# Sample-group attention of a one-step decoder: split float32r products over the whole array, or plain float32 products on 32-column quarters

## The chip, the cores and the metric

The kernel runs on one core of one Trainium2 chip. The metric is the device time of one execution in microseconds (us): the median of three runs before is 3056.04 us (3052.62 to 3064.1). Engines go by short names: PE (TensorE's matmuls), PEld (its weight loads), DVE (VectorE), ACT (ScalarE), POOL (GpSimd), SP (SyncE, which issues most DMAs). PSUM is the memory that PE writes.

## The reference, cut to what matters

One layer of a hybrid decoder runs for two groups of tokens with the same weights: a prompt of 512 tokens, and a sample group of 8 batches x 4 steps, 32 tokens. The change touches only work of the sample group:

```python
# stick-breaking attention, 8 heads x 128, 512 paged keys per batch and the 4 own ones
z = einsum('bqhd,bkhd->bhqk', q, k) * scale + b_h
survive = reverse_cumsum(log_stay) - log_stay
o = einsum('bhqk,bkhd->bqhd', exp(log_sigmoid(z) + survive), v)
# cross attention, 4 heads x 128, 256 memory keys per batch
attn = softmax(einsum('bshd,bmhd->bhsm', xq, mem_k) * 128 ** -0.5)
xo = einsum('bhsm,bmhd->bshd', attn, mem_v)
# gated delta rule: new state per batch and head
state = g_i * state + einsum('bhcd,bhce->bhde', k_i, v_new)
```

Everything is float32. Every batch has keys, values and states of its own, so each product with them has four query rows a head and no more.

## The kernel before, in words

**Dense work.** The projections hold 128 weight columns in the array and stream 544 tokens (prompt and sample) past them in two halves of 272. To have nearly float32's exactness from float32r operands, each operand is split into a high and a low part (`weights`, line 187; `split`, line 231), and three products are made: L208 (`products`) in the first half of the program, L1530 in the cross-attention's output projection, L1647 in the feed-forward part, where Winograd's scheme lowers the number of products.

**Side work.** All attention, of both groups, is written as Python generators that a class `Side` (line 391) hands out in small steps between the dense blocks. A step yields two estimates: PE time, and time until its results are there. `tick` is called after each dense block with that block's estimated PE time (0.68 us in `products`); it adds credit (that time times `ratio`) and runs steps while credit lasts, but a generator is picked again only when its estimated latency has gone by. So the yields set the order in which instructions are written, and a scheduler then fixes each engine's static order. `drain` runs what is left with nothing between.

**The sample group's attention.** `sb_sample` (line 575) does four heads, twice. It calls `sample_logits` (line 661) for two heads at a time, 16 units each of 256 keys, then `sample_values` (line 708) for 32 pages of 128 values. `cross_sample` (line 1424) calls the same two for the memory keys: twice 8 units, then 16 blocks of values. In all there are 80 units of logits, 64 pages of values and 16 blocks of memory values.

- A unit of logits: four PE transposes (L960) bring 256 keys of two heads to PSUM; `parts` (line 652) makes the high part (ACT cast, L656) and the low part (DVE subtraction, L657); four float32r matmuls of 256 columns (L699) multiply them. The stationary operand is a 128-column window of `win` that holds the high and the low part of the queries in the batch's eight columns and zeros elsewhere (POOL, L669 to L675), so all batches add up in one PSUM tile.
- A page of values: `parts` splits it the same way, then two float32r matmuls with 32 stationary columns and 512 streamed ones (L750). In `cross_sample` values are not split: one plain float32 matmul for a block.
- The two parts are summed by matmuls with 0/1 matrices: `selz` at L630 and L1460, `selv` at L757.

Pages go through a pool of seven tiles (`c.load`, tag `load`); SP issues their DMAs. In `sb_sample` a tile is free again when `parts` has read it.

**State update.** `gdn_sample` (line 1136) ends with 16 matmuls (L1246) for eight heads and two halves of the batches, each with 32 rows of the array (`tile_position=(hh * 32, 0)`), one in a step.

**Where it runs.** The two `sb_sample` generators are handed out from about 690 us on, between the last projections of `sb_project` and the gate projections; their last products stand at 1080 us. `cross_sample` runs between L1530's products of the first half of the tokens, and `side.drain()` finishes it before the second half begins (in `cross`, line 1482).

Of the kernel before, what the change touches and what calls it, by code (L numbers as in the profile page):

```python
# [15 lines left out]
P = 128  # L16
# [54 lines left out]
def build_consts(c):  # L71
# [45 lines left out]
    # rows (head of two, 7 - batch, part, step) to columns (head of two, batch, step), both parts summed  # L117
    c.selw = ones("selz", [P, 192], 0.0)
    c.selz = c.selw[:, 64:128]
    for part in range(2):  # L120
        sel(c.selz, [[-64, 2], [8, 8], [-1, 4]], 1, -56 - 4 * part, ALU.not_equal, 1.0)
    # rows (batch of four, part, head, step) to columns (head, batch of four, step): the head's own, both parts summed
    c.selv = ones("selv", [P, 64], 0.0)
    for part in range(2):
        sel(c.selv, [[-4, 4], [-32, 4], [-1, 4]], 1, -16 * part, ALU.not_equal, 1.0)
# [14 lines left out]
def head_rows(c):  # L140
    """Per-head scalars: columns (chunk, head) on every partition, and two columns with rows (head, batch, step)."""
# [45 lines left out]
def weights(c, w, k0, nk, c0, n=P, kept=False, eng=None):  # L187
    """A block of weights, split exactly into two parts of 12 bits each: a pair for every feature block."""
# [13 lines left out]
def products(c, ps, w, k, act, first, last, n=P):  # L202
    """One block of a projection: w^T act, exact but for the product of the two low parts."""
# [11 lines left out]
def project(c, w, k0, c0, acts, n=P, step=8):  # L215
    """PSUM [n, 2, 272] = (rows k0.. of w, columns c0..c0+n)^T acts"""
# [14 lines left out]
def split(c, x, g, hi=None, lo=None):  # L231
    """x * g (g per partition) as two exact parts."""
# [13 lines left out]
class Stats:  # L246
    """Sum of squares over all features, for every token, on every partition."""
# [15 lines left out]
    def rstd(self, name, scale=None):  # L263
        """(mean + EPS) ** -0.5; with scale, what was added is scaled by it, and so is the root's reciprocal."""
# [81 lines left out]
def x_rstd(c, ss):  # L346
    """The reciprocal roots of the tokens' mean squares, from columns to rows on every partition."""
# [21 lines left out]
def first_projections(c):  # L369
    """Loads the tokens and projects them on the first head's q and k, feature block by feature block."""  # L370
# [20 lines left out]
class Side:  # L391
    """Work of the mixers, handed out in small steps between the blocks of the projections.

    A step yields (tensor engine time, time until its results are there), both estimates in us."""
# [6 lines left out]
    def put(self, g, low=False, tiles=None):  # L401
        """tiles: where the work takes its temporary tiles (float32, float32r) from, if not from the usual ones"""
# [51 lines left out]
    def finish(self, e, steps=1e9):  # L454
        """Runs one work to its end, or until so many of its steps are done."""
# [5 lines left out]
    def drain(self, some=None):  # L461
        """Runs all that is left, or until some is done."""
# [70 lines left out]
    # the sums of the keys behind, a block of keys after the other, each token's in its own column  # L533
# [21 lines left out]
def stick(c, z, n, sp=None):  # L555
    """softplus(z) and log(sigmoid(z)), each over n columns"""
# [18 lines left out]
def sb_sample(c, g):  # L575
    """Stick-breaking attention of the sample group, four heads: 512 paged keys and its own."""
# [12 lines left out]
    # own keys: rows (head, batch, step)  # L589
# [28 lines left out]
    # paged keys: columns (page, head, batch, step)  # L618
    psz = c.aux()
    for h2 in range(2):  # L620
# [6 lines left out]
        nc.scalar.copy(zt[:, :512], ps)  # L627
        for p in range(PAGES):
            o = p * P + h2 * 64
            nc.tensor.matmul(psz[:, o : o + 64], zt[:, p * P : (p + 1) * P], c.selz, start=True, stop=True)  # L630
        yield 0.9
# [20 lines left out]
def parts(c, src, vector=True):  # L652
    """src [P, 512] as two exact parts."""
# [7 lines left out]
def sample_logits(c, q, h0, load, n, ps=None, col=0):  # L661
    """Products of two heads' queries (q: columns (head, batch, step)) with n blocks of 256 keys of every batch.

    Returns PSUM with rows (head, 7 - batch, part of q, step); load(b, i): [keys, (2 blocks, 2 heads, d)]."""
    nc = c.nc
    nb, win = 2, []
    for b0 in range(0, NB, nb):
        w = c.tp("win")
        nc.gpsimd.memset(w[:, : nb * 192].bitcast(F32), 0.0)  # L669
        for b in range(b0, b0 + nb):  # L670
            o = (b - b0) * 192 + (NB - 1 - b) * 8
            d = w[:, o : o + 256].rearrange("p (h x) -> p h x", h=2)
            x = q[:, h0 * 32 : (h0 + 2) * 32].rearrange("p (h b t) -> p h b t", h=2, b=NB)[:, :, b]
            nc.gpsimd.tensor_copy(d[:, :, 0:4], x)
            nc.gpsimd.tensor_sub(d[:, :, 4:8], x, d[:, :, 0:4].bitcast(F32))  # L675
            win += [[w[:, (b - b0) * 192 + hh * 64 :][:, :P] for hh in range(2)]]
        yield 0.0, 0.3
    first = ps is None
    if first:
        ps = c.aux()  # L680
# [3 lines left out]
    def ahead():  # L684
        if units:
            nxt.append(parts(c, transposes(c, load(*units.pop(0)))))
# [5 lines left out]
    for u in range(NB * n):  # L692
        b, i = divmod(u, n)
        k2 = nxt.pop(0)
        ahead()
        for hh in range(2):
            for j, k in enumerate(k2):
                o = col + i * 256
                nc.tensor.matmul(  # L699
                    ps[:, o : o + 256], win[b][hh], k.rearrange("p (g h k) -> p h g k", g=2, h=2)[:, hh],  # L700
                    start=first and u == 0 and hh == 0 and j == 0,
                    stop=b == NB - 1 and hh == 1 and j == 1, skip_group_check=True,
                )
        yield 0.9, 0.4
# [3 lines left out]
def sample_values(c, w, n, load, split=True):  # L708
    """Sums of n blocks of 128 values of every batch with the weights w (columns (block, head, batch, step)).

    With split, both are taken in two exact parts.

    Returns PSUM [d, (head, batch, step)]; load(b, i): [keys, (4 heads, d)]."""
    nc = c.nc
    win = []
    for i in range(0, n, 2):
        t = (c.tp if split else c.tt)("win")
        for j in range(2):
            x = w[:, (i + j) * P : (i + j + 1) * P].rearrange("p (h b t) -> p b h t", h=4, b=NB)
            d = t[:, j * 256 : (j + 1) * 256].rearrange("p (b u h t) -> p b u h t", b=NB, u=2, h=4)  # L720
            nc.scalar.copy(d[:, :, 0], x)
            if split:
                nc.vector.tensor_sub(d[:, :, 1], x, d[:, :, 0].bitcast(F32))
            else:
                nc.gpsimd.memset(d[:, :, 1], 0.0)
        win.append(t)
    yield 0.1
    pso = c.aux()
    units = [(b, i) for b in range(NB) for i in range(n)]
    nxt = []  # L730

    def ahead():
        if units:
            v = load(*units.pop(0))
            nxt.append(parts(c, v) if split else [v])

    ahead()
    ahead()
    ahead()
    yield 0.0  # L740
    for half in range(2):
        o = c.tt("os")
        for b4 in range(4):
            b = half * 4 + b4
            ps = c.aux()
            for i in range(n):
                vs = nxt.pop(0)
                for j, v in enumerate(vs):
                    x = (i % 2) * 256 + b * 32
                    nc.tensor.matmul(ps[:32], win[i // 2][:, x : x + 32], v, start=i == 0 and j == 0, stop=i == n - 1 and j == len(vs) - 1)  # L750
                ahead()
                yield 0.45, 0.4
            nc.scalar.copy(o[b4 * 32 : b4 * 32 + 32, :512], ps[:32])
        yield 0.0, 0.8
        for h in range(4):
            x = h * 32 + half * 16
            nc.tensor.matmul(pso[:, x : x + 16], o[:, h * P : (h + 1) * P], c.selv[:, h * 16 : h * 16 + 16], start=True, stop=True)  # L757
# [4 lines left out]
def load_pages(c, cache, pages, h0, nh):  # L762
    """[keys, (page, head, d)] of the given pages (indices into the table)."""
# [11 lines left out]
def gates(c, acts, rstd):  # L775
    """Decay and beta of the gated delta rule, with tokens on partitions."""
# [4 lines left out]
    # prompt: columns (a|b, chunk, head); sample: columns (a|b, stack), rows (head, batch, step)  # L781
# [28 lines left out]
    # running sums of log decay, totals, and their exponentials  # L810
# [22 lines left out]
    # per (head, batch) of the sample stacks, on every partition  # L833
# [7 lines left out]
def silu(c, x, out):  # L841
    """out = x * sigmoid(x), with exp and ln alone"""
# [1104 lines left out]
```

## Time and profile before

| | |
|---|---|
| median of 3 runs | 3056.04 us (3052.62 to 3064.1) |
| span of the profiled execution | 3059.9 us (its time beside that is not listed) |
| PE, PEld busy | 95%, 91% of the span |
| DVE, ACT, POOL busy | 70%, 45%, 55% |
| instructions on PE | 22118 matmul records |
| DMA | 392.67 MB, 128 GB/s over the span |
| mean granted TensorE clock | 0.983 |

A plain float32 matmul is one instruction of the program and two records in the profile (two passes, each with its own weight load); a float32r matmul or a transpose is one record. A record's duration includes the time until its results are written, which overlaps the next one; what a matmul costs a busy PE is the distance from its start to the next start. The timeline merges neighbours of one kind: a row gives the start of the first, the time to the end of the last, and their number.

### The profile page before, as it was taken

The numbers are of one execution on the slowest core, as the hardware profiler recorded it, in microseconds if no ns is written. First come the engines' busy times: TensorE is split into PE (matmuls) and PEld (weight loads), VectorE is DVE, ScalarE is ACT, GpSimd is POOL, SyncE is SP. The second block draws the span as 40 slices with busy tenths as digits, with TensorE's granted clock in tenths as the row PEclk, the third lists the DMA queues.
The fourth block names the chain that finished last, engine by engine and source line by source line (L and its number), as shares of the span: only waits on it lengthen the run. The fifth ranks groups of instructions, "written<-read, shape, count | busy, mean of one in ns | idle before, by whom it ended". The sixth has DMA issues, their size and how long they took to land.

```text
span 3059.9 us, 58347 instructions
## 1 busy us (share of the span) xinstructions
PE 2900.2 (95%) x22118; PEld 2789.1 (91%) x22118; DVE 2134.3 (70%) x3339; ACT 1363.5 (45%) x2600; POOL 1671.8 (55%) x1784
## 2 busy tenths in 40 slices
PE   8999999999999999999799999999999989988898
PEld 7999998889899999999689999999999989988797
DVE  6776775655655655366687777777777888888865
ACT  5544453435645654245543343333333344334333
POOL 3211122312112100032378988898888977999997
PEclk9999999999999999999899999999999999999999
DMA  7323233544535765423434344333434354344343
GB/s 212 95 80 85 75 88 99 144 137 147 173 105 151 227 197 150 127 81 116 161 117 127 118 122 123 121 117 118 125 118 123 116 179 132 110 131 127 119 137 105
DMA packets 619505, 392.67 MB, mean 128 GB/s; under 512 B 36475, under 2 KB 572360, under 8 KB 619224
## 3 DMA queue, kind: packets, MB, share of 16 engines
q1 hardware_dynamic: 596904, 355.95, 39.6%
q10 hardware_dynamic: 22320, 32.99, 3.0%
q8 instruction: 174, 2.85, 0.4%
q14 instruction: 107, 0.88, 0.1%
HBM read 334.17 MB, written 54.68 MB: 127 GB/s over the span
## 4 chain that ended last, share of the span: by engine, by line
POOL 27%; PE 20%; DVE 8%; issue 4%; DMA 4%; ACT 2%; SPq 0%; POOLq 0%; ACTq 0%; DVEq 0%
PE mm L208 7%; POOL u L1615 6%; POOL u L1613 6%; POOL u L1614 5%; PE mm L1647 5%; POOL u L1616 5%; PE aux L1647 4%; DVE wl L1621 3%; DMA u<-in_w_gate_up 2%; DVE pr L1591 2%; PE aux L1342 2%; POOL acc L1670 1%; PE mm L1530 1%; POOL x L1572 1%; PE aux L960 1%
## 5 line engine op out<-in xcount | busy, mean ns | idle before, releaser
L1621 DVE TENSOR_TENSOR wl<-u,wh 128x768 fp32r<-128x768 f32 (+1 forms) x528 | 752.5, 1442 | 315.9 <-ACT wh L1620 213.6
L1647 PE MATMUL mm<-pr,wh 128*128 128x272 f32 x4224 | 830.6, 292 | 41.6 <-DVE acc L1663 25.3
L1620 ACT CAST wh<-u 128x768 fp32r<-128x768 f32 (+1 forms) x528 | 488.8, 943 | 826.5 <-PE aux L1647 295.4
L1647 PEld LDWEIGHTS mm<-pr,wh 128*128 128x128 f32 x4224 | 669.4, 191 | 50.5 <-DVE acc L1663 20.3
L1647 PE MATMUL aux<-pr,wh 128*128 128x272 f32 x3168 | 626.9, 292 | 17.7 <-DVE acc L1669 6.7
L1647 PE MATMUL mm<-pr,wl 128*128 128x272 f32 x2112 | 615.7, 292 | 22.5 <-DVE wl L1621 22.5
L208 PE MATMUL mm<-ah,wh 128*128 128x272 f32 (+1 forms) x2464 | 538.6, 298 | 5.7 <-ACT ah L321 4.6
L1647 PEld LDWEIGHTS aux<-pr,wh 128*128 128x128 f32 x3168 | 506.8, 192 | 21.7 <-DVE acc L1669 8.6
L208 PE MATMUL mm<-al,wh 128*128 128x272 f32 (+1 forms) x2464 | 524.3, 291 | 0.7 <-DVE al L239 0.7
L208 PE MATMUL mm<-ah,wl 128*128 128x272 f32 (+1 forms) x2464 | 515.6, 290 | 0.1
L1647 PE MATMUL aux<-pr,wl 128*128 128x272 f32 x1584 | 460.9, 291 | 2.0 <-DVE wl L1621 2.0
L1647 PEld LDWEIGHTS mm<-pr,wl 128*128 128x128 f32 x2112 | 403.3, 191 | 28.4 <-DVE wl L1621 28.4
L208 PEld LDWEIGHTS mm<-ah,wh 128*128 128x128 f32 (+1 forms) x2464 | 391.9, 189 | 28.8 <-issue 8.5
L197 DVE TENSOR_TENSOR wl<-wr,wh 128x512 fp32r<-128x512 f32 (+1 forms) x366 | 264.0, 725 | 195.9 <-ACT wh L196 186.7
L208 PEld LDWEIGHTS mm<-al,wh 128*128 128x128 f32 (+1 forms) x2464 | 389.6, 188 | 5.4 <-issue 2.0
L208 PEld LDWEIGHTS mm<-ah,wl 128*128 128x128 f32 (+1 forms) x2464 | 386.2, 188 | 2.5 <-DVE wl L197 0.5
L196 ACT CAST wh<-wr 128x512 fp32r<-128x512 f32 (+1 forms) x366 | 224.3, 615 | 336.6 <-PE mm L208 272.6
L1613 POOL TENSOR_TENSOR u<-u 128x256 f32<-128x256 f32 x264 | 277.3, 1050 | 140.8 <-DMA u<-in_w_gate_up 90.2
L1615 POOL TENSOR_TENSOR u<-u 128x256 f32<-128x256 f32 x264 | 323.2, 1224 | 0.0
L1616 POOL TENSOR_TENSOR u<-u 128x256 f32<-128x256 f32 x264 | 308.5, 1169 | 19.1
L1647 PEld LDWEIGHTS aux<-pr,wl 128*128 128x128 f32 x1584 | 303.7, 192 | 2.6 <-DVE wl L1621 2.4
L1614 POOL TENSOR_TENSOR u<-u 128x256 f32<-128x256 f32 x264 | 270.4, 1024 | 0.0
(518 smaller groups left out, 3809.1 us busy)
## 6 DMA issues: line engine op xcount, KB each, us to landing
u<-in_w_gate_up SPq DMA_DIRECT2D x352, 256.0 KB
wr<-in_w_in SPq DMA_DIRECT2D x108, 512.0 KB
u<-in_w_down SPq DMA_DIRECT2D x176, 256.0 KB
v<-hT SPq DMA_DIRECT2D x66, 272.0 KB
page<-in_cache_sb_k SPq DMA_DIRECT2D x128, 128.0 KB
page<-in_cache_sb_v SPq DMA_DIRECT2D x64, 256.0 KB
wr<-in_w_out SPq DMA_DIRECT2D x32, 512.0 KB
hT<-x ACTq DMA_DIRECT2D x44, 272.0 KB
```

Of the source, the lines that this page charges most:

```text
L196: nc.scalar.copy(hi[:, :m, :n], raw[:, k : k + m, :n])
L197: nc.vector.tensor_sub(lo[:, :m, :n], raw[:, k : k + m, :n], hi[:, :m, :n].bitcast(F32))
L208: c.nc.tensor.matmul(ps[:n, h, :HT], l[:, :n], r[:, h * HT : (h + 1) * HT], start=first and i == 0, stop=last and i == 2,)
L1342: nc.tensor.matmul(ps[:, :256], l, r, start=k == 0 and n == 0, stop=k == 7 and n == 2)
L1591: nc.vector.tensor_sub(lo[:, o : o + n * HT], x[:, : n * HT], hi[:, : n * HT].bitcast(F32))
L1613: nc.gpsimd.tensor_add(s1, a21, a22)
L1614: nc.gpsimd.tensor_sub(s3, a11, a21)
L1615: nc.gpsimd.tensor_sub(s2, s1, a11)
L1616: nc.gpsimd.tensor_sub(s4, a12, s2)
L1620: nc.scalar.copy(hi, u[:, o : o + n])
L1621: nc.vector.tensor_sub(lo, u[:, o : o + n], hi.bitcast(F32))
L1647: nc.tensor.matmul(ps, l[:, cols], r, start=u + i == 0 and j == 0, stop=u + i == n - 1 and j == 2)
```

## The change

- **Logits.** Keys are no longer split: ACT copies the transposed keys (`kT`). For a unit, four plain float32 matmuls of 128 columns are issued, one for each quarter of 32 array columns (`tile_position=(0, x * 32)`): quarter x takes head x % 2 and block x // 2 of the keys. A quarter's stationary operand has 32 columns, the batch's four queries and 28 zeros. The window is made once for all batches, and the step after it yields (0.0, 3.0) where four steps yielded (0.0, 0.3).
- **Summing.** At L630's place two transposes take the place of four matmuls for each pair of heads. In `cross_sample` four matmuls with 64 array columns each take the place of two.
- **Values.** Pages are no longer split: a step takes four pages (two batches x two pages) in four plain float32 matmuls on the four quarters, straight from the DMA's tile. Five pages are asked for ahead, where three were. One ACT copy of 128 rows takes the place of four of 32 rows, and `selv`'s matmuls double in number (8 columns each, where it was 16).
- **State update.** Two heads' matmuls, on two different groups of 32 rows, stand next to each other.
- The file's comments are gone, so the change's line numbers are a little lower: L203 is L208 of before, L949 is L960, L1527 is L1530.

```diff
 def sample_logits(c, q, h0, load, n, ps=None, col=0):
...
+    w = c.tt("win")
+    nc.gpsimd.memset(w[:, :512], 0.0)
+    win = w[:, :512].rearrange("p (b h x) -> p b h x", b=NB, h=2)
+    for b in range(NB):
+        x = q[:, h0 * 32 : (h0 + 2) * 32].rearrange("p (h b t) -> p h b t", h=2, b=NB)[:, :, b]
+        nc.gpsimd.tensor_copy(win[:, b, :, b * 4 : b * 4 + 4], x)
+    yield 0.0, 3.0
...
-            nxt.append(parts(c, transposes(c, load(*units.pop(0)))))
+            pt = transposes(c, load(*units.pop(0)))
+            k = c.tt("kT")
+            nc.scalar.copy(k[:, :512], pt)
+            nxt.append(k)
...
-        k2 = nxt.pop(0)
+        k = nxt.pop(0)
+        o = col + i * P
+        for x in range(4):
+            nc.tensor.matmul(
+                ps[x * 32 : x * 32 + 32, o : o + P], win[:, b, x % 2, :], k[:, x * P : (x + 1) * P],
+                start=u == 0 and col == 0, stop=b == NB - 1, skip_group_check=True, tile_position=(0, x * 32),
+            )
         ahead()
-        for hh in range(2):
-            for j, k in enumerate(k2):
...
-        yield 0.9, 0.4
+        yield 0.7, 0.4
...
-def sample_values(c, w, n, load, split=True):
+def sample_values(c, w, n, load):
...
+    todo = [(b2 * 2 + b, i + j) for b2 in range(4) for i in range(0, n, 2) for b in range(2) for j in range(2)]
...
+    for _ in range(5):
+        ahead()
     yield 0.0
-    for half in range(2):
+    for b2 in range(4):
+        ps = c.aux()
+        for i in range(0, n, 2):
+            for g in range(4):
+                b, j = divmod(g, 2)
+                nc.tensor.matmul(
+                    ps[g * 32 : g * 32 + 32], win[i // 2][:, j, b2 * 2 + b], nxt[g], start=i == 0, stop=i == n - 2,
+                    skip_group_check=True, tile_position=(0, g * 32),
+                )
+            del nxt[:4]
+            for _ in range(4):
+                ahead()
+            yield 1.2, 0.6
         o = c.tt("os")
...
+        nc.scalar.copy(o[:, :512], ps)
         yield 0.0, 0.8
```

And in `gdn_sample`:

```diff
-    for hh in range(4):
...
+    for h2 in range(2):
         for w in range(2):
...
+            for hh, _, ps in two:
+                rows = slice(hh * 32, (hh + 1) * 32)
+                nc.tensor.matmul(
+                    ps, kn[rows, :], ex[w][rows].rearrange("p b d -> p (b d)"),
+                    start=True, stop=True, tile_position=(hh * 32, 0),
+                )
...
+            yield 1.2, 2.0
```

**Order, first place:** PE in the logits of the first four heads; L960 transposes the keys, L699 multiplies, L538 and L544 are another head's work. Before:

```order
L960 MATMUL aux<-ident,page 128x128 x4
L699 MATMUL aux<-part,win 128x256 x4
L544 MATMUL aux<-z,tri 128x128
L538 MATMUL aux<-sp,sfxr 128x256 x2
L960 MATMUL aux<-ident,page 128x128 x4
L699 MATMUL aux<-part,win 128x256 x4
```

With the change:

```order
L691 MATMUL aux<-kT,win 32x128 x4
L949 MATMUL aux<-ident,page 128x128 x4
L539 MATMUL aux<-z,tri 128x128
L533 MATMUL aux<-sp,sfxr 128x256 x2
L691 MATMUL aux<-kT,win 32x128 x4
L949 MATMUL aux<-ident,page 128x128 x4
```

The four matmuls of a unit stand together, between full-array work; that holds for all 80 units.

**Order, second place:** PE in the values of the last four heads (L750 before, L733 with the change). Before, a page's two matmuls stand after every six dense ones:

```order
L750 MATMUL aux<-part,win 32x512 x2
L208 MATMUL mm<-ah,wh 128x272 x2
L208 MATMUL mm<-al,wh 128x272 x2
L208 MATMUL mm<-ah,wl 128x272 x2
L750 MATMUL aux<-part,win 32x512 x2
```

With the change:

```order
L733 MATMUL aux<-page,win 32x512 x4
L203 MATMUL mm<-ah,wh 128x272 x2
L203 MATMUL mm<-al,wh 128x272 x2
L203 MATMUL mm<-ah,wl 128x272 x2
L733 MATMUL aux<-page,win 32x512 x3
L203 MATMUL mm<-ah,wh 128x272 x2
L203 MATMUL mm<-al,wh 128x272 x2
L203 MATMUL mm<-ah,wl 128x272 x2
L203 MATMUL mm<-ah,wh 128x272 x2
L733 MATMUL aux<-page,win 32x512
```

The step's four matmuls are partly torn apart: the 80 of them stand in 31 runs, 11 of one alone, 3 of two, 7 of three, 9 of four and 1 of six.

**Order, third place:** PE at the end of the cross attention of the sample group (L1530 or L1527 are the dense products there, L1460 or L1454 the summing, `ident,e` the transposes after the softmax). Before, dense products stand between all of these until the last 13 blocks of values:

```order
L1530 MATMUL mm<-xh,wl 128x272
L750 MATMUL aux<-xv,win 32x512 x5
L757 MATMUL aux<-selv,os 128x16 x4
L750 MATMUL aux<-xv,win 32x512 x8
L757 MATMUL aux<-selv,os 128x16 x4
L1530 MATMUL mm<-xh,wh 128x272 x2
```

With the change:

```order
L1527 MATMUL mm<-xh,wl 128x272
L691 MATMUL aux<-kT,win 32x128 x4
L949 MATMUL aux<-ident,xk 128x128 x4
L691 MATMUL aux<-kT,win 32x128 x4
L1454 MATMUL aux<-xz,ident 64x128 x4
L949 MATMUL aux<-ident,e 128x128 x2
L733 MATMUL aux<-xv,win 32x512 x4
L746 MATMUL aux<-selv,os 128x8 x4
L733 MATMUL aux<-xv,win 32x512 x6
L746 MATMUL aux<-selv,os 128x8 x4
L733 MATMUL aux<-xv,win 32x512 x3
```

The last two units of logits, the softmax and all values moved behind the last dense product of the first half of the tokens.

## Rows read from the trace of the kernel before

**Rows 1.** The page, part 1: busy time, share of the span, instructions.

```profile
PE 2900.2 (95%) x22118; PEld 2789.1 (91%) x22118; DVE 2134.3 (70%) x3339; ACT 1363.5 (45%) x2600; POOL 1671.8 (55%) x1784
```

**Rows 2.** By stretch: length, PE PEld DVE ACT POOL busy, clock, DMA share, GB/s.

```profile
690.00:1090.00 400.00, 388.18 (x2865) 359.79 (x2864) 240.24 (x398) 228.96 (x459) 78.07 (x161) 1.00 0.54 163
1420.00:1475.00 55.00, 52.94 (x333) 40.34 (x333) 24.64 (x52) 25.96 (x56) 16.19 (x37) 1.00 0.45 147
```

**Rows 3.** Waits of PE, 690 to 1090 us: total us, times, longest us.

```profile
PE aux L699 <- POOL win L675: 2.2, 1, 2.2
...
PE aux L750 <- DVE part L657: 1.6, 2, 1.1
PE aux L699 <- POOL win L674: 1.5, 1, 1.5
```

**Rows 4.** Groups by line and shape: busy us, mean ns | idle before.

```profile
L699 PE MATMUL aux<-part,win 128*128 128x256 f32 x320 | 60.2, 305 | 3.9 <-POOL win L675 2.2 <-POOL win L674 1.5 <-ACT part L656 0.3
...
L657 DVE TENSOR_TENSOR part<-aux,part 128x512 fp32r<-128x512 f32 x80 | 54.9, 690 | 33.1 <-ACT part L656 31.7 <-POOL win L675 0.8
...
L657 DVE TENSOR_TENSOR part<-page,part 128x512 fp32r<-128x512 f32 x64 | 44.9, 737 | 12.2 <-ACT part L656 12.1
L750 PE MATMUL aux<-part,win 128*32 128x512 f32 x128 | 42.2, 401 | 1.8 <-DVE part L657 1.6 <-ACT part L656 0.2
...
L750 PE MATMUL aux<-xv,win 128*32 128x512 f32 x32 | 14.7, 596 | 0.0
```

**Rows 5.** Timeline of PE, one unit of logits.

```profile
730.49 0.60 PE L960 MATMUL aux<-ident,page 128*128 128x128 f32 x4
730.84 0.72 PE L699 MATMUL aux<-part,win 128*128 128x256 f32 x4
731.40 0.41 PE L208 MATMUL mm<-ah,wh 128*128 128x272 f32 x2
```

**Rows 6.** Timeline of PE, one float32r matmul of the values between dense products.

```profile
848.64 0.28 PE L208 MATMUL mm<-ah,wl 128*128 128x272 f32 x1
848.76 0.39 PE L750 MATMUL aux<-part,win 128*32 128x512 f32 x1
848.99 0.29 PE L208 MATMUL mm<-ah,wl 128*128 128x272 f32 x1
```

**Rows 7.** Timeline of PE, plain float32 values of the cross attention and their summing.

```profile
1459.02 4.48 PE L750 MATMUL aux<-xv,win 128*32 128x512 f32 x10
1464.16 1.07 PE L757 MATMUL aux<-selv,os 128*128 128x16 f32 x8 [0.66 <-ACT os L753]
```

**Rows 8.** Timeline of PE, one state update on 32 rows.

```profile
536.78 0.39 PE L520 MATMUL aux<-hat,raw 128*128 128x128 f32 x2
537.10 1.12 PE L1246 MATMUL aux<-ex,kns 32*128 32x512 f32 x2
538.15 0.49 PE L1102 MATMUL aux<-ve,kn 128*128 128x128 f32 x2
```

**Rows 9.** Timeline of SP's queue, issues of pages of values.

```profile
1039.45 7.00 SPq L769 DMA_DIRECT2D page<-in_cache_sb_v  x9
```

**Rows 10.** Timeline of ACT, splitting those pages.

```profile
1044.74 1.29 ACT L656 CAST part<-page 128x512 fp32r<-128x512 f32 x2 [0.45 <-DMA page<-in_cache_sb_v]
```

**Rows 11.** Timeline of PE, summing the logits of the cross attention.

```profile
1445.25 1.03 PE L1460 MATMUL aux<-xz,selz 128*128 128x256 f32 x4
```

**Rows 12.** Timeline of DVE, the softmax behind it.

```profile
1446.59 0.42 DVE L1370 TENSOR_REDUCE sm<-aux 128x1 f32<-128x256 f32 x1
...
1448.28 0.35 DVE L1382 TENSOR_SCALAR e<-e,sm 128x256 f32<-128x256 f32 x1
```

**Rows 13.** Timeline of ACT, the weights of the values made from it.

```profile
1450.21 0.49 ACT L721 COPY win<-xat 128x128 f32<-128x128 f32 x2
```

**Rows 14.** PE by stretch: length, busy, then granted clock, DMA share, GB/s.

```profile
1480.00:1490.00 10.00, 10.00 (x82) 1.00 0.54 175
1490.00:1500.00 10.00, 4.31 (x29) 0.79 0.77 230
```

More of the change, by code (lines that the diff above doesn't have):

```diff
@@ L116, in build_consts @@
     blk(c.sel4, inner=1)
[L118 to L125, printed above, removed]
+    c.selv = ones("selv", [P, 32], 0.0)
+    for x in range(2):
+        sel(c.selv, [[-4, 4], [-64, 2], [-1, 4]], 1, -32 * x, ALU.not_equal, 1.0)
     c.id16 = ones("id16", [32, 256])
@@ L626, in sb_sample @@
         zt = c.tt("zt")
[L627 to L631, printed above, removed]
+        nc.scalar.copy(zt[:, :256], ps[:, :256])
+        for i in range(2):
+            out = psz[:, i * 256 : (i + 1) * 256].rearrange("p (a x) -> p a x", a=2)[:, :, h2 * 64 : h2 * 64 + 64]
+            nc.tensor.transpose(out, zt[:, i * P : (i + 1) * P], c.ident)
+        yield 0.25
     z = c.tt("z")
@@ L665, in sample_logits @@
     nc = c.nc
[L666 to L679, printed above, removed]
+    w = c.tt("win")
[5 more added lines that the diff above has]
+    yield 0.0, 3.0
+    if ps is None:
         ps = c.aux()
@@ L716, in sample_values @@
     for i in range(0, n, 2):
-        t = (c.tp if split else c.tt)("win")
+        t = c.tt("win")
+        d = t[:, :512].rearrange("p (j b u x) -> p j b u x", j=2, b=NB, u=2)
+        nc.gpsimd.memset(d[:, :, :, 1], 0.0)
         for j in range(2):
             x = w[:, (i + j) * P : (i + j + 1) * P].rearrange("p (h b t) -> p b h t", h=4, b=NB)
[L720 to L725, printed above, removed]
@@ L726, in sample_values @@
-        win.append(t)
+            nc.scalar.copy(d[:, j, :, 0].rearrange("p b (h t) -> p b h t", h=4), x)
+        win.append(d)
     yield 0.1
     pso = c.aux()
-    units = [(b, i) for b in range(NB) for i in range(n)]
+    todo = [(b2 * 2 + b, i + j) for b2 in range(4) for i in range(0, n, 2) for b in range(2) for j in range(2)]
     nxt = []
     def ahead():
[L733 to L738, printed above, removed]
@@ L739, in sample_values @@
-    ahead()
-    yield 0.0
-    for half in range(2):
-        o = c.tt("os")
[L743 to L753, printed above, removed]
+        if todo:
+            nxt.append(load(*todo.pop(0)))
@@ L754, in sample_values @@
         yield 0.0, 0.8
         for h in range(4):
-            x = h * 32 + half * 16
-            nc.tensor.matmul(pso[:, x : x + 16], o[:, h * P : (h + 1) * P], c.selv[:, h * 16 : h * 16 + 16], start=True, stop=True)
+            x = h * 32 + b2 * 8
+            nc.tensor.matmul(pso[:, x : x + 8], o[:, h * P : (h + 1) * P], c.selv[:, h * 8 : h * 8 + 8], start=True, stop=True)
         yield 0.9
@@ L1452, in load @@
             return t
-        ps = yield from sample_logits(c, f, h2 * 2, load, 1, ps if h2 else None, h2 * 256)
+        ps = yield from sample_logits(c, f, h2 * 2, load, 1, ps if h2 else None, h2 * P)
     z = c.tt("xz")
-    nc.scalar.copy(z[:, :512], ps)
+    nc.scalar.copy(z[:, :256], ps[:, :256])
     yield 0.0, 1.5
@@ L1459, in cross_sample @@
     for h2 in range(2):
-        nc.tensor.matmul(ps[:, :256], c.selw[:, 64 - h2 * 64 :][:, :P], z[:, h2 * 256 : h2 * 256 + 256], start=h2 == 0, stop=h2 == 1)
+        for k in range(2):
+            nc.tensor.matmul(
+                ps[h2 * 64 : h2 * 64 + 64, k * P : (k + 1) * P], c.ident[:, k * 64 : k * 64 + 64], z[:, h2 * P : (h2 + 1) * P],
+                start=k == 0, stop=k == 1, skip_group_check=True, tile_position=(0, h2 * 64),
+            )
     e = softmax(c, ps, 1)
@@ L1470, in loadv @@
         return t
-    pso = yield from sample_values(c, at, 2, loadv, False)
+    pso = yield from sample_values(c, at, 2, loadv)
     o = c.tt("xo")
```

30 lines of the change are left out of this document (10 added, 20 removed).

## The prediction

> **What bounds the kernel now.** I read the page first, then the two stretches in which the sample group's attention runs, then the waits of PE there, and then distances between starts on PE's timeline.
>
> The page says that PE is the bound: busy 95% of the span, no other engine over 70% [rows 1]. Busy overstates it, since records overlap, so I asked stretch by stretch. In the 400 us of paged attention PE is busy 388 us and DVE 240, at full clock; in the cross attention's stretch PE 53 of 55 us and DVE 25 [rows 2]. So the removed splitting is not what PE lacks time for: the 144 DVE subtractions of 55 + 45 us and the casts beside them run under PE's work, and their going gains only where PE waited for them. The waits show how little: 2.2 + 1.5 us for the windows of queries, 1.6 us for a split page [rows 3]. The change is therefore mostly a question of PE's own time in logits, values and sums, whose records are few among 22118 [rows 4].
>
> **PE's time, part by part.** Costs are start-to-start distances.
>
> *Logits, 80 units.* A unit takes 730.49 to 731.40, 0.91 us: four transposes of 0.11 and 0.47 for four float32r matmuls [rows 5]. A float32r matmul of 512 columns costs 0.23 (848.76 to 848.99) [rows 6]; a pass of a plain float32 one costs 0.43: ten records end after 4.48 us, the last lasting about 0.6 as the group's mean says, so nine distances take 3.88 [rows 4, 7]. For 128 columns a pass is a quarter, 0.107, and the unit's four matmuls are eight passes. One after the other they take 0.86 against 0.47; if all quarters ran at once, 0.22. No row before shows two quarters at work, so these are the bounds.
>
> I take a value between. Each instruction is two passes on the same quarter, and rows of one quarter show the second starting only when the first has streamed, 0.43 later [rows 7]. The timeline's matmuls start in the order in which they are issued. So the second pass of a quarter can run beside the first pass of the next, and no more: n matmuls take n + 1 passes instead of 2n, four take 5 x 0.107 = 0.54. For each hand-over I add 0.03, a quarter of the 0.1 that a first, uncovered load of 128 weight columns costs: the state update's two records end after 1.12 us, the last lasting 0.59, so their starts lie 0.53 apart, not 0.43 [rows 8]. A unit's four then cost 0.63: 80 x (0.63 - 0.47) = +13 us (all at once with hand-overs -14, without -20; in series +31).
>
> The Trainium skill, page "TensorE: Matmul & The Clock Gate", Part 3, says the same of the order (matmuls start and end in program order), but also that three column tiles gave 2.38 times the speed; by that figure the unit's four would take some 0.3 us, an estimate for single-pass matmuls that no row here bears out.
>
> *Values.* Before: 128 x 0.23 + 32 x 0.43 = 43.2 us. With the change 80 instructions in 31 runs: (80 + 31) passes x 0.43 + 49 hand-overs x 0.03 = 49.2, so +6 (all at once: 31 x 0.86 + 1.5 = 28, -15; in series 160 x 0.43 = 69, +26).
>
> *State updates.* One between full-array work costs 0.3 us beyond its 0.86: the 128-column float32 matmul before it starts at 536.78 and takes 0.22, the update starts at 537.10, not 537.00, and the next full one at 538.15, not 537.96 [rows 8]. Before: 16 x 0.86 + 14 runs x 0.3 = 18; with the change 8 pairs x (3 x 0.43 + 0.03 + 0.3) = 13, so -5 (all at once -8, in series -2).
>
> *Sums.* `selv` gains 24 instructions, 48 passes of 0.115 (eight records end after 1.07, the last lasting 0.26) [rows 7]: +5.5. `selz` loses 16, 32 such passes (3.7), for 8 transposes of 0.11: -2.8. L1460's replacement comes out even.
>
> Together +17 us on PE.
>
> **Waits.** The windows' and the split pages' waits go: -5 [rows 3]. What is late next is the page itself. Its tile was freed by `parts`; now PE reads it, and the eighth page of a pair of batches can be asked for only when the first of the seven tiles has been read. Nine pages are issued from 1039.45 on, and ACT waits until 1044.74 for one [rows 9, 10]: if it is the first of them, a page lands 5 us after its issue (the row leaves 2 to 7). Eight pages with the dense products between them take some 10.5 us by my costs, so most of that is covered: +4 (0 to 12). SP issues the dense weights in the same queue behind these pages; three weight tiles cover about 15 us, so I cost that at nothing.
>
> The larger new wait stands at the end of the cross attention. The yield of 3.0 us, twice, pushes the last logits, softmax and all values behind the last dense product of that half, as the third place of the order shows; in-order PE then waits for the chain that dense products covered. It runs from the end of the summing, 1445.25 + 0.86 [rows 11], over the reduction at 1446.59 and the scaling at 1448.28 [rows 12] to the end of the weights' copies, 1450.70 [rows 13]: 4.6 us. The copies of the last keys, of the logits and one more of the partial values add about 0.7 each, after the 0.66 that such a copy costs PE now [rows 7]. That is 6.7. Around the idle stretch at 1490 us the granted clock falls to 0.79 in the mean of 10 us, part of it at 1.2 GHz of 2.4 [rows 14]; I add 1. In all +8 (5 to 11).
>
> **Sum.** 17 - 5 + 4 + 8 = +24. The profiled span is 3059.9 us, 3.9 above the median of the runs; its own time beside the span isn't listed. 3059.9 + 24 = 3084 by the span; on the median of 3056 that is **3080 us**. With the open terms (hand-overs 0 to 0.06, pages, tail) this case alone reaches from 3060 to 3098.
>
> **Rivals.**
> *All four quarters at once (faster).* If a quarter queues its second pass while others start, PE's terms become -17 (between -14 and -20), -15, -8 and +3: -37. The windows' -5 stays. Values then go faster than pages land: a step of eight takes some 8.3 us and waits about 1.5, +12 in all. Tail +7. Sum -23: **3033**. For it: separate quarters have separate columns and PSUM partitions. Against it: two passes of one quarter in a row, and matmuls started in order. It decides if a run of four 128-column matmuls takes under 0.35 us.
>
> *No overlap (the change doesn't do what it says).* In series: +31 + 26 - 2 + 3 = +58, waits -5, pages 0, tail +9: +62, **3118**. For it: the trace has no two tiles at work together. Against it: nothing but that quarters share no column.
>
> *A price for each switch (slower).* State updates pay 0.3 us to leave and re-enter the full array [rows 8]. If quarters pay it too, the 80 runs of logits and 31 of values add 33 us to the forecast's case: **3113**. Against it: L750 already uses a quarter's 32 columns, the first, and enters 0.12 after a dense product that costs 0.12, and leaves after 0.23, its own cost [rows 6]. By that it is free; only the other quarters are untried. The Trainium skill, page "TensorEngine Tiling (Array Packing)", Tiling Modes, states that a change of tiling mode drains TensorE; the state updates agree, at 0.3 us, while L750's rows don't.
>
> **How the numbers follow.** Forecast 0.40, all at once 0.33, no overlap 0.14, switches 0.13. I call a difference within 0.5%, 15 us, no change: about what a measurement of this kernel can tell. Faster (under 3041): eight in ten of the second case, 0.27, and 0.03 of the first: 0.30. Same: 0.06 of the second case and a third of the first, 0.13: 0.19. Slower: 0.51. The range from 3022 to 3112 takes in nearly all of the first two cases and leaves out some half of the last two and a little of the second below it, under 0.2.
>
> **What would show it.** On PE's timeline a unit's four matmuls (L691) should span about 0.63 us to the next full-array start; under 0.35 is the second case, 0.86 the third, 0.9 the fourth. Runs of four in L733 should take 2.2 us (0.9 or 3.4 in the rivals). DVE should fall by 100 us without PE idling less than 5 us fewer. Before the values of the cross attention PE should stand idle for over 4 us, with a stretch of lower clock. The forecast is wrong if these hold and the time still isn't near 3080: then dense products lost or gained time, through weights queued behind pages on SP.

## The result, and the profile after

The changed kernel takes 3073.9 us (median of 5 runs, 3070.05 to 3076.3) beside 3059.92 us for the kernel before in the same comparison: a ratio of 1.0045, with a 95% interval of 1.0029 to 1.006. That is 14 us slower. The forecast was 3080 us, 24 above the median of 3056 then known. The size was near, but several of the steps that led to it were wrong and made up for each other, as the rows show, so that the nearness is in part luck.

The page of the changed kernel, part 1:

```profile
PE 2891.8 (94%) x22466; PEld 2746.9 (90%) x22466; DVE 2042.7 (67%) x3187; ACT 1322.7 (43%) x2524; POOL 1658.8 (54%) x1718
```

DVE lost 92 us of work (2134.3 in [rows 1]) and ACT 41; the forecast named 100 for DVE. Yet the span grew from 3059.9 to 3068.3 us. To see where, I took the start of the same dense product in both traces: the changed kernel is 0.8 us late at 520 us, 1.7 **early** at 1130, after all state updates and the paged attention, 2.4 early at 1404, and 10.9 **late** at 1475 us of the trace before; the difference then stays between 10 and 12 until 1790 and is 8.6 at the end. So the paged attention gained a little, and the cross attention of the sample group lost some 13 us.

**Logits.** The timeline of PE after, two units with six dense products between (columns: start, time to the end of the last, engine, line, operation and number of records):

```profile
730.11 0.42 PE L691 MATMUL aux<-kT,win 128*32 128x128 f32 x8
730.47 0.66 PE L949 MATMUL aux<-ident,page 128*128 128x128 f32 x4
730.88 0.50 PE L203 MATMUL mm<-ah,wh 128*128 128x272 f32 x2
731.22 0.41 PE L203 MATMUL mm<-al,wh 128*128 128x272 f32 x2
731.46 0.41 PE L203 MATMUL mm<-ah,wl 128*128 128x272 f32 x2
731.80 0.43 PE L691 MATMUL aux<-kT,win 128*32 128x128 f32 x8
```

The four matmuls span 0.36 us to the next full-array start, not 0.63: the quarters run at once. But their neighbours pay: two dense products after the transposes start 0.34 apart where 0.25 is usual, and the last two before the run likewise. A whole turn takes 731.80 - 730.11 = 1.69; less six dense products (0.75) and four transposes (0.44) that is 0.50 for a run, while two passes of 0.107 would be 0.21. So each run has a price of about 0.29 us. Before, a turn with the same four transposes and six dense products took 1.66: from 730.49 [rows 5] to the next unit's start, here:

```profile
732.15 0.60 PE L960 MATMUL aux<-ident,page 128*128 128x128 f32 x4
```

A unit thus costs 0.03 more than before, and 80 of them 2 us. (One of the 80 units stands torn in two in the trace, at 762 us.)

**Values.** PE after: one run of four matmuls and its turn, then one of a lone matmul and its turn:

```profile
1035.19 1.07 PE L733 MATMUL aux<-page,win 128*32 128x512 f32 x8
1036.18 0.52 PE L203 MATMUL mm<-ah,wh 128*128 128x272 f32 x2
1036.54 0.41 PE L203 MATMUL mm<-al,wh 128*128 128x272 f32 x2
1036.79 0.41 PE L203 MATMUL mm<-ah,wl 128*128 128x272 f32 x2
1037.13 0.62 PE L733 MATMUL aux<-page,win 128*32 128x512 f32 x2
...
1051.25 1.05 PE L733 MATMUL aux<-page,win 128*32 128x512 f32 x2
1052.23 0.40 PE L203 MATMUL mm<-ah,wh 128*128 128x272 f32 x1
1052.46 0.42 PE L203 MATMUL mm<-al,wh 128*128 128x272 f32 x2
1052.71 0.41 PE L203 MATMUL mm<-ah,wl 128*128 128x272 f32 x2
1052.97 0.29 PE L203 MATMUL mm<-ah,wh 128*128 128x272 f32 x1
1053.18 1.04 PE L733 MATMUL aux<-page,win 128*32 128x512 f32 x2
```

Both turns take 1.93 to 1.94 us, and both hold six dense products: a run costs 1.18 us whether it has one matmul or four. That is two passes of 0.43 and a price of 0.32. Of the 31 runs, 11 hold one matmul alone.

**The state update.** PE after, two pairs with six dense products between:

```profile
621.56 1.13 PE L1237 MATMUL aux<-ex,kns 32*128 32x512 f32 x4
622.62 0.52 PE L203 MATMUL mm<-ah,wh 128*128 128x272 f32 x2
622.98 0.41 PE L203 MATMUL mm<-al,wh 128*128 128x272 f32 x2
623.22 0.41 PE L203 MATMUL mm<-ah,wl 128*128 128x272 f32 x2
623.56 1.13 PE L1237 MATMUL aux<-ex,kns 32*128 32x512 f32 x4
```

The pair costs 2.00 - 0.75 = 1.25 us, as much as a single one did (1.05 to the next start [rows 8], and about 0.2 in its neighbours). Two groups of rows run at once as well.

**The tail of the cross attention.** PE after, around the last dense products of the first half; rows of dense products are left out, but for the first of the second half:

```profile
1448.16 0.63 PE L949 MATMUL aux<-ident,xk 128*128 128x128 f32 x4 [0.86 <-DMA xk<-in_cache_mem_k]
...
1458.23 0.43 PE L691 MATMUL aux<-kT,win 128*32 128x128 f32 x8
1460.68 0.63 PE L949 MATMUL aux<-ident,xk 128*128 128x128 f32 x4 [2.02 <-DMA xk<-in_cache_mem_k]
1462.07 0.66 PE L691 MATMUL aux<-kT,win 128*32 128x128 f32 x8 [0.77 <-ACT kT L679]
1463.21 1.13 PE L1454 MATMUL aux<-xz,ident 128*64 128x128 f32 x8 [0.48 <-ACT xz L1448]
1466.39 0.66 PE L949 MATMUL aux<-ident,e 128*128 128x128 f32 x2 [2.06 <-DVE e L1374]
1467.95 2.08 PE L733 MATMUL aux<-xv,win 128*32 128x512 f32 x8 [0.89 <-issue]
1470.77 1.87 PE L746 MATMUL aux<-selv,os 128*128 128x8 f32 x8 [0.75 <-ACT os L742]
...
1475.93 1.06 PE L746 MATMUL aux<-selv,os 128*128 128x8 f32 x8
...
1485.42 0.82 PE L1527 MATMUL mm<-xh,wh 128*128 128x272 f32 x2 [0.63 <-ACT xh L1475]
```

From 1458.23 to 1485.42 no dense product stands between. PE waits for the softmax, as forecast, but also for pages of keys, which the forecast had not seen. And the granted clock falls: the eight records of L746 take 1.87 us at 1470.77, at 1.2 GHz, and 1.06 at 1475.93, at 2.4 GHz. From 1400 us to the first dense product of the second half, the views before and then after read (length, busy time of PE, PEld, DVE, ACT, POOL, clock, DMA share, GB/s):

```profile
1400.00:1475.00 75.00, 70.80 (x447) 56.67 (x446) 35.86 (x79) 37.57 (x90) 19.55 (x54) 0.98 0.50 159
1400.00:1486.00 86.00, 69.79 (x511) 52.68 (x510) 26.46 (x62) 35.00 (x85) 15.30 (x35) 0.84 0.43 135
```

PE waits 16 us in this stretch, 4 before. The clock stands at 1.2 GHz for 27 us of it, 3 before. In 6 of the 27 PE waits anyway, and half of the rest is lost: about 10 us, against 2 before (an estimate from the trace's record of the clock). Waits and clock together cost some 20 us more, for a loss of 13, so PE's own work there has become cheaper by about 7.

The last five pages of keys are asked for one at a time now; two of them on SP's queue after:

```profile
1443.72 0.45 SPq L1441 DMA_DIRECT2D xk<-in_cache_mem_k  x1
...
1448.21 0.45 SPq L1441 DMA_DIRECT2D xk<-in_cache_mem_k  x1
```

Before, 11 of them were asked for in a row, and the last of these pages was transposed only at 1439.5 us:

```profile
1412.67 6.96 SPq L1449 DMA_DIRECT2D xk<-in_cache_mem_k  x11
```

The reason can be read in the code: `cross_sample` gets the rings of the projections' operands, a ring of 16 tiles for `c.tt` and one for `c.tp`. The split parts came from `c.tp`; the new copies `kT` come from `c.tt`, as do the pages of keys. Whether this or the yields of 3.0 made the tail is what the first two experiments tell apart.

### The profile page after: what moved, and what is told of

The parts are those of the page before. It is cut to its first block, busy times and chain, and to the rows that moved or that the text cites. A ratio compares the mean times of both kernels' runs of the same rounds, so it can differ in the third digit from the quotient of the medians.

```text
span 3068.3 us, 58577 instructions
## 1 busy us (share of the span) xinstructions
PE 2891.8 (94%) x22466; PEld 2746.9 (90%) x22466; DVE 2042.7 (67%) x3187; ACT 1322.7 (43%) x2524; POOL 1658.8 (54%) x1718
## 4 chain that ended last, share of the span: by engine, by line
PE 39%; POOL 29%; DVE 13%; DMA 6%; issue 6%; ACT 4%; SPq 1%; POOLq 0%; ACTq 0%; DVEq 0%
PE mm L203 19%; POOL u L1612 7%; POOL u L1610 6%; POOL u L1611 6%; POOL u L1613 5%; PE mm L1644 4%; DVE wl L1618 3%; PE aux L1644 3%; DMA u<-in_w_gate_up 3%; PE aux L949 2%; DVE pr L1588 2%; PE aux L1334 2%; PE aux L733 1%; DVE p L869 1%; POOL acc L1667 1%
## 5 line engine op out<-in xcount | busy, mean ns | idle before, releaser
L203 PE MATMUL mm<-ah,wh 128*128 128x272 f32 (+1 forms) x2464 | 545.3, 301 | 7.0 <-ACT ah L316 3.5
L203 PE MATMUL mm<-al,wh 128*128 128x272 f32 (+1 forms) x2464 | 523.0, 291 | 0.0
L203 PE MATMUL mm<-ah,wl 128*128 128x272 f32 (+1 forms) x2464 | 514.0, 290 | 0.1
L203 PEld LDWEIGHTS mm<-ah,wh 128*128 128x128 f32 (+1 forms) x2464 | 387.5, 188 | 39.3 <-issue 26.2
L203 PEld LDWEIGHTS mm<-al,wh 128*128 128x128 f32 (+1 forms) x2464 | 388.5, 188 | 6.1 <-issue 3.8
L203 PEld LDWEIGHTS mm<-ah,wl 128*128 128x128 f32 (+1 forms) x2464 | 385.1, 188 | 2.1 <-DVE wl L192 0.5
```

The costliest lines, as they stand in the source:

```text
L203: c.nc.tensor.matmul(ps[:n, h, :HT], l[:, :n], r[:, h * HT : (h + 1) * HT], start=first and i == 0, stop=last and i == 2,)
```

## The experiments

Ratios are to the kernel before, with their 95% intervals.

**ring.** The copies take the other ring:

```diff
-            k = c.tt("kT")
+            k = c.tp("kT").bitcast(F32)
```

> The changed kernel with one edit: the copies of the transposed keys take their tiles from the other ring (the one that the split parts used before), so that in the cross attention of the sample group they no longer share a ring of 16 tiles with the pages of keys. Theory 'ring': the 10 us that the changed kernel loses between 1450 and 1486 us come from pages of keys that are asked for one at a time, because the copies hold their tiles; then the last logits, the softmax and the first values stand between dense products again, PE waits for no page of keys (5.6 us in the changed kernel), and the time falls by 9 to 12 us, to about 3063. Theory 'yield' (the prediction's): the two yields of 3.0 push the work back; then nothing changes, 3074 within 4 us.

Measured: 3060.02 us, ratio 1.0003 (0.9994 to 1.0012), 14 us below the changed kernel, a little more than expected, and no longer to be told from the kernel before. PE in `ring`, the same place, without the dense products:

```profile
1445.25 0.43 PE L691 MATMUL aux<-kT,win 128*32 128x128 f32 x8
1448.43 0.67 PE L1454 MATMUL aux<-xz,ident 128*64 128x128 f32 x8
1452.15 0.38 PE L949 MATMUL aux<-ident,e 128*128 128x128 f32 x2
1456.24 1.04 PE L733 MATMUL aux<-xv,win 128*32 128x512 f32 x2
```

The logits end at 1445 instead of 1462 us, the softmax lies under dense products, and no wait for a page of keys is left. In this stretch PE waits 7 us instead of 16, and the granted clock is back at a mean of 0.98 (0.84 in the changed kernel). SP asks for 11 pages in a row again:

```profile
1414.56 8.53 SPq L1441 DMA_DIRECT2D xk<-in_cache_mem_k  x11
```

**yl.** The yields as they were:

```diff
-    yield 0.0, 3.0
+    for _ in range(4):
+        yield 0.0, 0.3
```

> The changed kernel with one edit: after the window of queries is made, the step yields (0.0, 0.3) four times, as before the change, instead of (0.0, 3.0) once. Theory 'yield' (the prediction's): the tail of the cross attention gets its cover of dense products back, and the time falls by 8 to 10 us, to about 3065. Theory 'ring' (pages of keys are late, because the copies of transposed keys hold the ring's tiles): nothing changes there, 3074 within 4 us, and PE still waits for pages of keys by about 5 us.

Measured: 3069.58 us, ratio 1.0042 (1.0026 to 1.0057), not to be told from the changed kernel's 1.0045, though 4 us below it. PE's waits in `yl` between 1395 and 1500 us (total us, times, longest):

```profile
PE aux L950 <- DMA xk<-in_cache_mem_k: 6.0, 4, 3.0
```

So the tail was made by the ring, not by the yields. The forecast had the right place and the wrong cause, and its 8 us for waits and clock stand beside some 20.

**q0.** The logits on one quarter:

```diff
+            y = x * 32 if b == 0 else 0
             nc.tensor.matmul(
-                ps[x * 32 : x * 32 + 32, o : o + P], win[:, b, x % 2, :], k[:, x * P : (x + 1) * P],
+                ps[y : y + 32, o : o + P], win[:, b, x % 2, :], k[:, x * P : (x + 1) * P],
...
-                tile_position=(0, x * 32),
+                tile_position=(0, y),
```

> The changed kernel with one edit: the four matmuls of a unit of logits all go to the first quarter of the array, for all batches but the first (70 of 80 units), so that the logits of heads and blocks are added into one another. Theory 'all at once' (four quarters stream at the same time, and a run costs two passes and a price of about 0.3 us): in one quarter the four take eight passes of 0.107 one after the other, 0.86 where it was 0.21, a unit 0.64 longer: +45 us, about 3119. Theory 'no overlap' (the quarters ran one after the other anyway): 3074. The prediction's case, five passes for four matmuls: 0.32 longer, +22 us, 3096.

Measured: 3110.25 us, ratio 1.0165 (1.0149 to 1.018): 36 us above the changed kernel. PE in `q0`, a unit:

```profile
730.01 1.06 PE L692 MATMUL aux<-kT,win 128*32 128x128 f32 x8
731.00 0.66 PE L950 MATMUL aux<-ident,page 128*128 128x128 f32 x4
```

The run spans 0.99 us where it was 0.36, the 0.64 that was expected: on four quarters the four were at work at once. 56 of the 70 units lie in the paged attention, 56 x 0.64 = 36 us, and the same dense product at 1400 us starts 37 us later than in the changed kernel. What the 14 units of the cross attention should have added (9 us) doesn't show at the end: the delay grows to 43 us by 1445 us of the trace before and is back at 38 by 1475, behind a tail in which PE waits 1.6 us for pages of keys instead of 5.6. This share was not looked into further.

**dep.** A step's four matmuls of values kept together, by an order of issue alone:

```diff
-            for g in range(4):
+            first = None
+            for g in (3, 0, 1, 2):
...
+                if first is None:
+                    first = m.ins
+                else:
+                    c.tc.add_manual_dep(m.ins, first.name, NOSYNC, reason="together")
```

> The changed kernel with one edit: the four matmuls of a step of values are kept together in PE's order, 21 runs of them instead of 31. Theory 'price per run': a run of one to four matmuls on different quarters costs the same, 0.98 us and 0.2 in its neighbours, since all quarters stream at once and the array pays some 0.3 us for each run; ten runs fewer give 12 us back, less up to 5 us of waits for pages, so about 3062 to 3067. Theory 'per matmul' (each matmul costs, wherever it stands): no change, 3074 within 4 us.

Measured: 3074.79 us, ratio 1.0045 (1.0031 to 1.0059): no gain, as the theory 'per matmul' would have it. Only the trace tells them apart. The runs in the paged attention fell from 27 to 17, and each still costs what a lone matmul did (1.00 us to the next start, 0.98 for a lone one), so PE's own time fell by about 12 us there; but it now waits for whole steps of pages (`dep`, 690 to 1095 us):

```profile
PE aux L737 <- DMA page<-in_cache_sb_v: 4.9, 5, 1.9
```

The same wait was 0.3 us in the changed kernel. The clock took about as much: in `dep` it falls to 1.2 GHz three times between 690 and 1130 us, 3.4 us each (a mean of 0.91 in 940 to 960, 1045 to 1065 and 1095 to 1115 us), where the changed kernel has 1.00 throughout; PE works all the while, so some 5 us are lost. At 1130 us the dense products of `dep` run 3.4 us earlier than the changed kernel's, about what 12 - 5 - 5 leaves. That lead is gone by 1665 us, in work that the edit doesn't touch, which I have not explained. For the time by itself this run is inconclusive.

**ringungdn.** `ring`, with the state update of before:

```diff
-    for h2 in range(2):
+    for hh in range(4):
         for w in range(2):
...
-            yield 1.2, 2.0
+            yield 0.9
```

> The kernel 'ring' (3060) with the state update as it was before the change: one matmul on 32 rows in a step, 16 of them. Theory 'term': a pair costs 1.06 us and 0.2 in its neighbours where two single ones cost 2.5, so eight pairs had saved some 9 us, and the time rises to 3069. Theory 'given back': the pairs' steps brought waits of PE with them (7.4 us between 525 and 692 us, 1.1 before the change), so undoing them costs only what is left, 2 to 4 us: about 3063, and PE's waits in this stretch fall below 3 us. The prediction's term was 5.

Measured: 3069.7 us, ratio 1.0032 (1.0021 to 1.0043), 9 to 10 us above `ring`. The time is what 'term' said, but the trace bears out 'given back'. PE's waits between 525 and 692 us fell from 7.4 to 2.1 us, since these rows of `ring` (and of the changed kernel, among others) are gone:

```profile
PE aux L1147 <- POOL sqk L840: 2.8, 1, 2.8
PE aux L1261 <- POOL css L1259: 1.3, 2, 1.1
```

At its place the edit costs 3 us: the dense products of `ringungdn` are 0.6 us later than those of `ring` at 520 us, before the state updates, and 3.8 later from 750 to 820. That is the pairs' 9 us less the 5 to 6 of waits that they brought. The rest arises where nothing was edited: the traces stand 7.5 us apart at 1130, 9 at 1475 and 14 at the end (the profiled execution of `ringungdn` took 3074.7 us, 5 above its median). The clock has a part in it, as in 945 to 965 us with a mean of 0.91 where `ring` has 1.00; the whole was not taken apart, and how much of the 9 to 10 us belongs to the pairs stays open.

**ringpair.** `ring`, with two units of logits in a run (for that, four units are transposed ahead instead of two, and the yields change a little):

```diff
-    for u in range(NB * n):
+    for u2 in range(0, NB * n, 2):
+        for u in (u2 + 1, u2):
...
+                if last is not None:
+                    c.tc.add_manual_dep(m.ins, last.name, NOSYNC, reason="together")
+                last = m.ins
```

> The kernel 'ring' (3060) with the logits of two units next to each other, eight matmuls in a run, two on each quarter. Theory 'price per run': two runs of four cost 0.50 us each beside dense work (two passes of 0.107 and some 0.29 for the run); one run of eight costs four passes and one price, 0.72, so a pair saves 0.28 and 40 of them 11 us: about 3049, a run of eight spanning 0.57 us. Theory 'per matmul' (the price hangs on each matmul or its weights): no change, 3060 within 4 us.

Measured: 3057.16 us, ratio 0.9997 (0.9988 to 1.0006), 3 us below `ring`. The time is as 'per matmul' expected, but the run itself does what 'price per run' expected:

```profile
724.11 0.65 PE L695 MATMUL aux<-kT,win 128*32 128x128 f32 x16
724.69 0.66 PE L958 MATMUL aux<-ident,page 128*128 128x128 f32 x4
```

0.58 us for eight matmuls, 0.36 for four: only two more passes of 0.107. But the order of the values changed with it: they stand in 32 runs in the paged attention where `ring` had 27, 17 of them alone where it had 11. Five runs at 1.18 are 6 us of the 11; the remaining 2 were not looked for.

**ringdeppair.** `ring` with the edits of `ringpair` and `dep`, so that values cannot be torn apart.

> The kernel 'ring' (3060) with both edits: logits of two units next to each other, and the four matmuls of a step of values kept together. By the price per run 11 us from the logits; from the values what 'dep' kept of its 12 us after PE's waits for pages (5 us there) and whatever else, 0 to 6: 3043 to 3049. PE waits for pages of values by 4 to 6 us again.

Measured: 3047.87 us, ratio 0.9965 (0.9952 to 0.9977). That is 12 us below `ring`, as expected, and 9 below `ringpair`; PE waits 6.7 us for pages of values, a little more than expected. Values stand in 16 runs in the paged attention, where `ringpair` had 32.

**best.** `ringdeppair`, with pages of values in two rings and eight asked for ahead:

```diff
-    t = c.load("page")
+    t = (c.tt if nh == 4 and pages[0] % 2 else c.load)("page")[:, :512]
...
-    for _ in range(5):
+    for _ in range(8):
```

> The kernel 'ringdeppair' with pages of values in two rings of tiles in turn (7 of the pages' own and free ones of the general ring) and eight pages asked for ahead instead of five. If the gain of keeping a step's matmuls together was lost to late pages, PE's waits for them fall under 1 us and the time is 4 to 6 us below 'ringdeppair', about 3040. If it was lost elsewhere, the two take the same time within 3 us.

Measured: 3037.65 us, ratio 0.9934 (0.992 to 0.9948), faster than both kernels: 36 us below the changed one. PE's wait for pages of values, 690 to 1095 us:

```profile
PE aux L743 <- DMA page<-in_cache_sb_v: 1.5, 1, 1.5
```

The gain on `ringdeppair` is 10 us, where 4 to 6 were expected. Five are these waits; where the other 5 come from was not taken apart. The two traces differ by 3 us already at 200 us, before any edited line runs, so a few us between two single traces say little.

## Why the prediction was right, and where its steps were wrong

The range held the time and its sign was the forecast's. By the forecast's own measure, though, 14 us is still "no change", to which it gave 0.19. The working fares less well.

**Two passes beside each other.** The forecast's first step, that a second pass waits and four matmuls take five passes, is wrong. The signs it named read 0.36 us for a unit (0.63 forecast, under 0.35 for the second case) and 1.0 us for a run of four values (2.2 forecast, 0.9 for the second case). `q0` shows it from the other side. The rival 'all four quarters at once' had the mechanism.

The sign at the tail held: right before the values PE idles 6 us, at a lowered clock.

**A price for each switch.** The forecast gave the fourth case 0.13, because L750 entered and left a quarter's 32 columns for nothing [rows 6]. Those rows are float32r. The plain float32 form of the same line stood in the same trace, between dense products (PE before):

```profile
1453.01 0.29 PE L1530 MATMUL mm<-xh,wl 128*128 128x272 f32 x1
1453.23 1.04 PE L750 MATMUL aux<-xv,win 128*32 128x512 f32 x2
1454.20 0.39 PE L1530 MATMUL mm<-xh,wh 128*128 128x272 f32 x1
1454.43 0.29 PE L1530 MATMUL mm<-xl,wh 128*128 128x272 f32 x1
```

Start to start that is 0.22, 0.97 and 0.23, where 0.126, 0.86 and 0.126 would be free: 0.31 us for one run on the first quarter. I read only the middle of such a row, ten matmuls in a series [rows 7], in which the price is spread over ten.

The obvious rival is that the price is one of plain float32 among float32r products, and not of the narrow tile. The same trace speaks against it. Here L520, plain float32 on the full array, stands between dense products (PE before):

```profile
705.02 1.02 PE L520 MATMUL aux<-hat,raw 128*128 128x512 f32 x2
705.47 0.81 PE L208 MATMUL mm<-ah,wh 128*128 128x272 f32 x2
706.12 0.41 PE L208 MATMUL mm<-al,wh 128*128 128x272 f32 x2
```

From 705.02 to 706.12 is 1.10; less two dense products (0.25) that is 0.85, its two passes and no price. Of the forms that were seen here, only plain float32 in a narrow tile pays. The Trainium skill, page "TensorEngine Tiling (Array Packing)", Tiling Modes, says that a change of tiling mode drains TensorE; the plain float32 runs agree with that, at about 0.3 us each, the float32r ones of 32 columns don't.

**The sum by these two.** The second case's -23 us with the fourth's 111 runs at 0.3 gives +10, and the time was +14. Each of the two cases that stood alone, 3033 and 3113, was far off; no case of mine held both. That +10 comes near is luck too: the second case held +12 for late pages, of which 0.3 came.

**Terms.** Logits: +13 forecast, 80 x 0.03 = +2 measured. Values: +6 forecast; 31 x 1.18 = 37 against 128 x 0.23 and, for the 16 plain ones in five runs, 16 x 0.86 and 5 x 0.31, together 45: -8. State updates: -5 forecast; eight at 1.25 against twelve at 1.25 and two runs of two at 2.1 give -9; 6 us of new waits around the state updates, which were not forecast, give most of it back, and `ringungdn` differs by 3 at this place. Sums: +3 forecast, not measured by itself. PE's waits between 690 and 1090 us fell from 12 to 8 us, near the 5 forecast. Page waits: +4 forecast, 0.3 there; `dep` shows that the same pages cost 5 when the runs are kept whole.

**By stretch.** For states and paged attention the forecast's terms add up to about +16 (logits +10, values +11, states -5, sums +1, waits -5, pages +4); the trace shows -2.5 (0.8 late to 1.7 early), near the measured +2, +2, -9, +1 as forecast, and +2 of waits. For the cross attention they add up to about +8 (logits +3, values -5, sums +2, tail +8); the trace shows +12.5: about 12 more of waits, 8 of lower clock, and -7 of PE's own work, since the values there cost 10 less. The tail's 6.7 of waits were too small, and its 1 for the clock far too small.

There the step "the yield of 3.0 us, twice, pushes the last logits ... behind the last dense product" failed: `yl` undid it without effect, `ring` took the loss away. The step that was missing is the ring from which a new tile comes.

**Why the number was near.** The forecast had +17 for PE's own work and +7 for waits and clock. By the costs above (with the +3 for sums as forecast), PE's own work came to about -12, and waits and clock to about +22 (-4, +6, +12 and +8). Two errors, of 29 us down and 15 up, left the time in the range. That is luck, not a sign that the mechanism was right.

**Dense weights behind the pages on SP**, costed at nothing: PE's waits for `wh` in the paged attention are the same 0.5 us before and after.

## What to carry to other kernels

Small plain float32 matmuls on separate quarters ran at once here, but each run of them that stands alone between full-array work pays its price: count runs, not matmuls, and put as many as possible into each. When an edit gives a tile a new name or type, look up which ring it now comes from and what else lives there; here pages that lost their free tiles made PE wait up to 2.4 us for one, far from the edited line, and the clock fell with the waits. And look in the trace for the row of the same line in the same number format and in the same surroundings before deciding that something is free.

## What the runs showed of the hardware

- One to four plain float32 matmuls of 512 columns, each on its own quarter of 32 columns, span 0.98 to 1.00 us to the next full-array start, less than 0.01 for each further one; four of 128 columns span 0.36, eight (two for each quarter) 0.58, and four on one quarter 0.99.
- A run of plain float32 matmuls on 32 columns or 32 rows costs 0.3 to 0.4 us beyond its passes between full-array products, however many it holds. Plain float32 on the full array pays nothing of the kind (0.85 for two passes of 0.43), and neither does a float32r matmul with 32 columns on the first quarter, beyond its own 0.23. Which part of a run's price is entering, leaving or weights was not separated, and float32r on the other quarters was not tried.
- The tail in which PE waits 16 us of 84 has a mean clock of 0.84; with the waits gone (`ring`, 7 of 69) it is 0.98. The same eight records take 1.87 us at 1.2 GHz and 1.06 at 2.4.
